# A decode step of a hybrid layer on one core: low products moved to the end of each unit, one head's convolution moved to VectorE

## The chip, the core and the metric

The kernel runs on one core of a Trainium2 chip, in one launch. Its time is the device time of an execution in microseconds (us). TensorE is called PE here, VectorE DVE, ScalarE ACT, GpSimd POOL and SyncE SP, as in the profile. Every engine works off its own list of instructions in order; a wait for another engine or for a DMA stops that list.

## The reference

One layer of a decoder trunk for 256 prompt and 64 sample tokens (8 sequences of 8), 320 columns in all, with a model width of 2048, in fp32:

```
h = rmsnorm(x)
proj = h @ w_in                       # 2048 x 3072: a_val, a_gate, b_u, b_v, c_u
z = a_val * sigmoid(a_gate)           # A: 4 heads of 128 channels
out_a = silu(layernorm_heads(depthwise_conv31(concat[state, z]) + conv_b))
out_b = b_u * (tril(w_s) @ layernorm(b_v) + b_s)          # B: 4 heads of 128
out_c = s5(c_u)                       # C: 64 groups of 16 channels, a complex diagonal SSM, then a GLU
x = x + concat[out_a, out_b, out_c] @ w_out
g, u = split(rmsnorm(x) @ w_gu)       # 2048 x 11264
x = x + (silu(g) * u) @ w_down        # 5632 x 2048
y = rmsnorm(x)
```

Returned are y, the convolution's last 30 positions, the SSM's last states and the layer-normed b_v rows of the samples. The depthwise convolution has 31 taps per channel: each output position is the sum of 31 shifted copies of the row, each with its channel's weight.

## The kernel before

**Products.** Activations lie with channels on partitions and the 320 tokens along the row. Every weight matrix comes from memory as tiles of 128x1024 fp32 (a *unit*: eight 128x128 blocks, `j` = 0 to 7). To keep fp32 accuracy a product is made of three passes: ACT rounds the weights to `hi` (line 208), DVE makes the remainder `lo` = raw - hi (line 217, recorded as L52, the line of the helper through which all DVE work goes), and the activation rows are kept as a high and a low part as well. For block `j` PE does `hi` x high row (L237), `hi` x low row (L238) and `lo` x high row (L240), all into one PSUM tile `acc`. In `mm` (line 232) a unit is done in four quarters of two blocks: four matmuls with `hi`, then two with `lo`.

**Order.** Loads, splits and products of unit u+3, u+2, u+1 and u are issued side by side from one loop over the units. `ORDER` (line 26) lists the units of the mixers after the first eight: C0 to C7 are the SSM's inputs, A2 and A3 the convolution heads 2 and 3 (heads 0 and 1 come first), K0 to K3 the convolutions of the four heads, U0 to U3 and V the two halves of B. After them come 16 output tiles for the C channels (`post_oc`), 16 for A and B, the gate/up tiles and the down tiles.

**Work beside the products.** The mixers' own work is written as generators (`Task`). `Side.run` is called after each quarter of a unit. Tasks of priority below 1 are stepped whenever they are due; `Wait(n)` makes a task due n quarters later. Tasks of priority 1 and up (the SSM's recurrence, layer norms, B's gating) are stepped while the estimated time of the DVE work issued so far (`vec.t`) is not above that of the PE work (`pe`, line 131). `side.until(cond)` steps every task that is due, without that limit, until the condition holds. All of this happens while the program is built: it fixes the order of each engine's list, and not a time.

**Convolution.** `conv_in` (line 544) writes a head's row to DRAM and reads it back four times, shifted, into `z4` (32 channels x 4 shifts on 128 partitions, issued from POOL). `k_mm` (line 565) then does the 31 taps as eight groups of four on PE with 32x32 diagonal weights `cwd`; `k_post` adds the bias.

**The C chain.** `c_out` (three PE products per group) gives `z`, ACT applies gelu, `z_layout` (line 927) turns it through DRAM (`dz`, then four reads into `zc`, all issued from SP), `c_glu` (line 937) does two PE products, ACT the tanh, DVE the product `oc`, ACT its high part `oh` and DVE its low part `ol`. The first C output tile needs all eight such pairs of rows (`crows`).

**End.** After the last product the final norm's factor multiplies 16 rows of `xa`: rows 12 to 15 on POOL (two operations), the others on DVE, with seven stores (line 1366).

## Time and profile before

| what | us |
|---|---|
| median of 3 runs | 1352.18 (1348.64, 1352.18, 1353.87) |
| the profiled execution | 1352.68 |
| its span, first to last instruction | 1351.0 |
| PE busy in the span | 1318.4 |
| DVE busy | 721.8 |
| ACT busy | 565.8 |
| PE idle in the first 296 us, all of it | 18.3 |
| PE idle between 296 us and the last down product | 0.0 |

The profile is of one execution. Its time stands against the span: 1.7 us lie outside. The idle time of PE was read off the timeline row by row (waits of 0.3 us and more; the last of them before the final norm ends at 295.15 us). A busy PE is not always a PE at full speed: the granted clock is 1.00 in nearly every stretch, and lower in a few of the first 225 us.

### The profile page before, as it was taken

To read this page: it belongs to the slowest core of one execution; us is meant where nothing else is said; L and a number is where in the kernel's file an instruction comes from. 1 tells how busy PE (TensorE), PEld (TensorE's weight loads), DVE (VectorE), ACT (ScalarE), POOL (GpSimd) and SP (SyncE) were. 2 spreads that over 40 slices of the span, in tenths; PEclk is the share of its full clock that TensorE was granted. 3 is DMA by queue.
4 is the path that set the end of the run, shared out by engine and by line. 5 is a ranking of instruction groups with operands and counts; after the bars stand their busy time and mean duration, and the time that the engine had idled before them with its cause. 6 is when DMAs were issued, how large, how long until landed. Compare 5 with 4: busy or idle time off the path is not lost.

```text
span 1351.0 us, 22667 instructions
## 1 busy us (share of the span) xinstructions
PE 1318.4 (98%) x9324; PEld 1290.4 (96%) x9324; DVE 721.8 (53%) x1195; ACT 565.8 (42%) x824; POOL 71.9 (5%) x101
## 2 busy tenths in 40 slices
PE   8999999999999999999999999999999999999995
PEld 8888987899999999999999999999999999999995
DVE  8867986685555444444444444444444444434444
ACT  7378535474454333333333333333233333322452
POOL 1110101010130000000000000000000000000112
PEclk9999998999999999999999999999999999999998
DMA  7784576564444554444444444555444445554453
GB/s 261 194 204 133 142 187 161 168 210 141 149 147 142 175 173 148 148 141 157 155 146 151 141 157 155 147 150 152 146 156 145 152 141 158 155 148 141 142 152 121
DMA packets 78584, 212.49 MB, mean 157 GB/s; under 512 B 20640, under 2 KB 28064, under 8 KB 78416
## 3 DMA queue, kind: packets, MB, share of 16 engines
q1 hardware_dynamic: 71440, 198.34, 46.6%
q0 software_dynamic: 6176, 10.94, 3.2%
q8 instruction: 73, 1.20, 0.4%
q10 hardware_dynamic: 864, 1.76, 0.3%
q14 instruction: 31, 0.25, 0.1%
HBM read 203.47 MB, written 8.73 MB: 157 GB/s over the span
## 4 chain that ended last, share of the span: by engine, by line
PE 90%; DVE 4%; DMA 3%; ACT 2%; issue 1%; SPq 0%; DVEq 0%; ACTq 0%
PE acc L240 28%; PE acc L237 28%; PE acc L238 28%; DMA raw<-in_win 2%; DVE lo L52 1%; PE acc L577 1%; PE sc L758 1%; PE sc L914 1%; PE acc L1018 1%; PE sc L915 1%; PE sc L916 1%; PE acc L1020 1%; PE acc L1019 1%; PE sc L770 0%; ACT hi L208 0%
## 5 line engine op out<-in xcount | busy, mean ns | idle before, releaser
L52 DVE TENSOR_TENSOR lo<-raw,hi 128x1024 fp32r<-128x1024 f32 (+1 forms) x357 | 421.3, 1181 | 213.5 <-issue 164.0
L208 ACT ACTIVATE hi<-raw 128x1024 fp32r<-128x1024 f32 (+2 forms) x361 | 369.3, 1024 | 340.1 <-PE acc L238 246.5
L237 PE MATMUL acc<-hh,hi 128*128 128x320 f32 x1408 | 424.4, 309 | 0.0
L238 PE MATMUL acc<-hl,hi 128*128 128x320 f32 x1408 | 422.8, 308 | 0.0
L240 PE MATMUL acc<-hh,lo 128*128 128x320 f32 x1408 | 321.0, 308 | 0.0
L237 PEld LDWEIGHTS acc<-hh,hi 128*128 128x128 f32 x1408 | 264.4, 188 | 0.1
L238 PEld LDWEIGHTS acc<-hl,hi 128*128 128x128 f32 x1408 | 264.4, 188 | 0.1
L240 PEld LDWEIGHTS acc<-hh,lo 128*128 128x128 f32 x1408 | 234.7, 188 | 0.0
L237 PE MATMUL acc<-fh,hi 128*128 128x320 f32 x704 | 212.0, 309 | 0.0
L238 PE MATMUL acc<-fl,hi 128*128 128x320 f32 x704 | 211.8, 308 | 0.0
L240 PE MATMUL acc<-fh,lo 128*128 128x320 f32 x704 | 165.5, 308 | 0.0
L237 PEld LDWEIGHTS acc<-fh,hi 128*128 128x128 f32 x704 | 132.2, 188 | 0.0
L238 PEld LDWEIGHTS acc<-fl,hi 128*128 128x128 f32 x704 | 132.1, 188 | 0.0
L240 PEld LDWEIGHTS acc<-fh,lo 128*128 128x128 f32 x704 | 118.9, 188 | 0.0
L52 DVE TENSOR_TENSOR xa<-acc,xa 128x320 f32<-128x320 f32 x80 | 39.3, 491 | 127.8 <-PE acc L240 127.8
L237 PE MATMUL acc<-xh,hi 128*128 128x320 f32 x288 | 91.2, 324 | 2.0 <-ACT hi L208 2.0
L1210 ACT ACTIVATE fh<-fu 128x320 fp32r<-128x320 f32 x44 | 20.8, 472 | 163.0 <-DVE fu L52 163.0
L238 PE MATMUL acc<-xl,hi 128*128 128x320 f32 x288 | 87.8, 312 | 0.0
L1188 ACT ACTIVATE fg<-fg 128x320 f32<-128x320 f32 x44 | 20.8, 472 | 138.9 <-DVE fg L52 138.9
L52 DVE TENSOR_TENSOR fu<-acc,rs 128x320 f32<-128x320 f32 x44 | 21.6, 492 | 98.0 <-PE acc L240 98.0
L52 DVE TENSOR_TENSOR fg<-acc,rs 128x320 f32<-128x320 f32 x44 | 21.6, 492 | 95.9 <-PE acc L240 95.9
L240 PE MATMUL acc<-xh,lo 128*128 128x320 f32 x288 | 66.9, 314 | 4.4 <-DVE lo L52 4.4
(255 smaller groups left out, 1353.5 us busy)
## 6 DMA issues: line engine op xcount, KB each, us to landing
raw<-in_wgu SPq DMA_DIRECT2D x176, 512.0 KB, 3.5
raw<-in_wdn SPq DMA_DIRECT2D x80, 512.0 KB, 3.6
raw<-in_win SPq DMA_DIRECT2D x37, 512.0 KB, 4.5
raw<-in_wout SPq DMA_DIRECT2D x32, 512.0 KB, 3.5
z<-zr POOLq DMA_DIRECT2D x16, 296.0 KB, 12.6
raw<-in_wv SPq DMA_DIRECT2D x8, 512.0 KB, 4.2
raw<-in_wdn SPq DMA_DIRECT2D x16, 256.0 KB, 2.6
xa<-in_xT SPq DMA_DIRECT2D x4, 640.0 KB, 7.5
```

Source lines behind the costliest of these rows:

```text
L52: return self.v.tensor_tensor(out, a, b, op=op)
L208: A.activation(d["hi"][:, o], d["raw"][:, o], AF.Copy)
L237: T.matmul(ps, hi[:, c], r[u + j][0], start=u + j == 0, stop=False)
L238: T.matmul(ps, hi[:, c], r[u + j][1], start=False, stop=False)
L240: T.matmul(ps, lo[:, j * 128:j * 128 + 128], r[u + j][0], start=False, stop=u + j == n - 1)
L577: T.matmul(ps[c, o:o + n], w[:, 32 * (8 * g + j):32 * (8 * g + j) + 32], x, start=j == 0, stop=j == 7, tile_position=(0, 32 * g))
L758: T.matmul(pe[:, 80 * p:80 * p + 80], ps[ri][:, p, :], U[:, ct, p, :], start=True, stop=True)
L914: T.matmul(o, cat(bd[:, 0, p, 1:5]), H[:, 0, 4 * i + p, 0:80], start=True, stop=False)
L915: T.matmul(o, cat(bd[:, 1, p, 1:5]), H[:, 1, 4 * i + p, 0:80], start=False, stop=False)
L916: T.matmul(o, Tt[:, p, :], U[:, i, p, :], start=False, stop=True)
L1188: A.activation(gs, gs, AF.Silu)
L1210: A.activation(h, ub, AF.Copy)
```

## The change

Seven edits. Where a block of eight had been worked off in four quarters of `hi, hi, hi, hi, lo, lo`, the unit's 16 products with `hi` now come first and its eight with `lo` last. K3 is gone from `ORDER`: the fourth head is convolved in `conv_v` on DVE, 31 taps of one operation on 256 and one on 64 columns, as a task of priority 3.5; its weights are a small table `cw`, and its row goes to the output straight from SBUF. `conv_in` waits two quarters before each of its four shifted reads. `Side.run` lets DVE's estimate run 2.0 us ahead of PE's. `dz` is written from ACT's queue at once; the reads back come five quarters later instead of four, and are due after four instead of three. `b_load` comes after head 2's convolution. The last 16 rows are all multiplied on DVE, in six operations, with six stores.

```diff
-ORDER = "C0 C1 C2 C3 K0 C4 C5 C6 C7 K1 A2 U0 A3 U1 K2 V K3 U2 U3".split()
+ORDER = "C0 C1 C2 C3 K0 C4 C5 C6 C7 K1 A2 U0 A3 U1 K2 V U2 U3".split()
...
-        while self.vec.t <= self.pe:
+        while self.vec.t <= self.pe + 2.0:
...
-                for j in range(a, b):
-                    c = slice(j * 128, j * 128 + 128)
-                    T.matmul(ps, hi[:, c], r[u + j][0], start=u + j == 0, stop=False)
-                    T.matmul(ps, hi[:, c], r[u + j][1], start=False, stop=False)
-                for j in range(a, b):
-                    T.matmul(ps, lo[:, j * 128:j * 128 + 128], r[u + j][0], start=False, stop=u + j == n - 1)
+                todo = [(hi, j, i) for j in range(m) for i in range(2)] + [(lo, j, 0) for j in range(m)]
+                for w, j, i in todo[3 * a:3 * b]:
+                    T.matmul(ps, w[:, j * 128:j * 128 + 128], r[u + j][i], start=w is hi and u + j + i == 0,
+                             stop=w is lo and u + j == n - 1)
...
-            side.add(0.3, conv_in(h))
+            if h < 3:
+                side.add(0.3, conv_in(h))
+            else:
+                side.add(3.2 + 0.1 * h, conv_v(h))
...
         for g in range(4):
+            yield Wait(2)
             G.dma_start(z4[:, g], bass.AP(tensor=base.tensor, offset=base.offset + 32 * g * ZW,
                                            ap=[[1, 4], [ZW, 32], [1, Z4]]))
+
+    def conv_v(h):
+
+        row, cw = S["row", h], S["cw"]
+        G.dma_start(O["rows"][h], row)
+        while "cw" not in S or S["of"] >= 7:
+            yield Wait(1)
+        S["of"] += 1
+        f = tmp("of", bufs=7)
+        fs = f[:, NP:].rearrange("p (s t) -> p s t", s=8)
+        for k in range(31):
+            w = cw[:, k:k + 1]
+            for o, x in ((f[:, 0:NP], row[:, k:k + NP]), (fs, samples(row)[:, :, k:k + 8])):
+                if k == 0:
+                    V.tensor_scalar(o, x, w, cv[:, h, 0:1], op0=MULT, op1=ADD)
+                else:
+                    V.scalar_tensor_tensor(o, x, w, o, op0=MULT, op1=ADD)
+            yield None
+        S["k", h] = True
+        side.add(0.9, mix_a(h, f))
...
-            if h == 3:
+            if h == 1:
+                side.until(lambda: "src" in S)
+                cw = S["cw"] = tmp("kk", (128, 64))
+                G.dma_start(cw[:, 0:32], I["cw"])
+            if h == 2:
                 b_load()
...
-        yield Wait(2)
-        nc.sync.dma_start(dz, z)
-        yield Wait(4)
+        nc.scalar.dma_start(dz, z)
+        yield Wait(5)
         for p in range(4):
             nc.sync.dma_start(zc[32 * p:32 * p + 32], dz[:, p, :].rearrange("(j g) q -> g j q", j=4))
-        S["z due", i] = side.now + 3
+        S["z due", i] = side.now + 4
...
-        if u in (100, 102, 104, 106):
+        if u in (100, 102, 104):
...
-    for E, q, a, b in ((G, 3, 0, 2), (G, 3, 2, 4), (V, 0, 0, 1), (V, 0, 1, 4), (V, 1, 0, 4), (V, 2, 0, 3), (V, 2, 3, 4)):
-        E.tensor_tensor(rows(q, a, b), rows(q, a, b), r[:, None, :].to_broadcast([128, b - a, NT]), op=MULT)
-    for E, q, a, b in ((nc.sync, 0, 0, 1), (nc.scalar, 0, 1, 4), (nc.sync, 3, 0, 2), (nc.scalar, 1, 0, 4),
-                       (nc.sync, 3, 2, 4), (nc.scalar, 2, 0, 3), (nc.sync, 2, 3, 4)):
-        E.dma_start(O["yT"][:, 4 * q + a:4 * q + b, :], rows(q, a, b))
+    for n, (q, a, b) in enumerate(((0, 0, 1), (0, 1, 4), (1, 0, 4), (2, 0, 4), (3, 0, 3), (3, 3, 4))):
+        V.tensor_tensor(rows(q, a, b), rows(q, a, b), r[:, None, :].to_broadcast([128, b - a, NT]), op=MULT)
+        (nc.scalar if n % 2 else nc.sync).dma_start(O["yT"][:, 4 * q + a:4 * q + b, :], rows(q, a, b))
```

What this does to the engines' lists, at the three places that the next sections speak of.

**PE, from the last quarters of U3 to the first C output tile.** Before, `sc<-zc,wg` (the two GLU products of a group) and `sc<-z,wv` (B's mixing product of a head) have parts of U3 (`acc<-xh,hi` and so on) between them; `sm<-of` is a sum for the layer norm of a convolution head:

```order
L606 MATMUL sm<-of,ones_113 128x320
L237 MATMUL acc<-xh,hi 128x320
L238 MATMUL acc<-xl,hi 128x320
L237 MATMUL acc<-xh,hi 128x320
L238 MATMUL acc<-xl,hi 128x320
L240 MATMUL acc<-xh,lo 128x320 x2
L1064 MATMUL sc<-z_3185,wv 128x128
L1065 MATMUL sc<-z_3185,wv 128x128
L1066 MATMUL sc<-z_3185,wv 128x64
L949 MATMUL sc<-zc,wg 128x320
L950 MATMUL sc<-zc,wg 128x320
L1064 MATMUL sc<-z_3185,wv 128x128
```

Now the same place reads:

```order
L237 MATMUL acc<-xh,lo 128x320 x6
L974 MATMUL sc<-zc,wg 128x320
L975 MATMUL sc<-zc,wg 128x320
L1089 MATMUL sc<-z_2586,wv 128x128
L1090 MATMUL sc<-z_2586,wv 128x128
L1091 MATMUL sc<-z_2586,wv 128x64
L624 MATMUL sm<-of,cent 128x320
L974 MATMUL sc<-zc,wg 128x320
L975 MATMUL sc<-zc,wg 128x320
L1089 MATMUL sc<-z_2586,wv 128x128
L1090 MATMUL sc<-z_2586,wv 128x128
L1091 MATMUL sc<-z_2586,wv 128x64
```

With K3 gone the units end sooner in the list: the last two GLU products and the last two mixing products stand behind the whole of U3, with no unit's products between them, and the first C output tile follows at once.

**DVE, at the end of V.** Before, the recurrence's last addition (`H<-lnv`) is followed by the reads of V's sums (`wv<-acc`):

```order
L52 TENSOR_TENSOR lnv<-lnv,H 128x256
L52 TENSOR_TENSOR H<-lnv 128x2x16x8
L61 TENSOR_SCALAR wv<-acc,rc 128x512
L52 TENSOR_TENSOR wv<-acc,wv 64x512
L52 TENSOR_TENSOR lo<-raw,hi 128x1024
```

Now six taps (`of<-row,kk`, a 256 and a 64 each) stand between them; here the last two of them:

```order
L56 SCALAR_TENSOR_TENSOR of<-row,kk,of 128x256
L56 SCALAR_TENSOR_TENSOR of<-row,kk,of 128x64
L56 SCALAR_TENSOR_TENSOR of<-row,kk,of 128x256
L56 SCALAR_TENSOR_TENSOR of<-row,kk,of 128x64
L61 TENSOR_SCALAR wv<-acc,rc 128x512
L52 TENSOR_TENSOR wv<-acc,wv 64x512
L52 TENSOR_TENSOR lo<-raw,hi 128x1024
```

**DVE, before the last low C row.** Now, from the product `oc` of group 7 to its low row `ol<-oc,oh`:

```order
L56 SCALAR_TENSOR_TENSOR oc<-g_3440,g_3439 128x4x80
L56 SCALAR_TENSOR_TENSOR of<-row,kk,of 128x256
L56 SCALAR_TENSOR_TENSOR of<-row,kk,of 128x64
L52 TENSOR_TENSOR gs<-sc,z_2586 128x256
L52 TENSOR_TENSOR gs<-sc,z_2586 128x64
L56 SCALAR_TENSOR_TENSOR of<-row,kk,of 128x256
L56 SCALAR_TENSOR_TENSOR of<-row,kk,of 128x64
L52 TENSOR_TENSOR ol<-of,oh 128x320
L52 TENSOR_TENSOR ol<-oc,oh 128x320
```

Before, the same two had an inverse square root's two operations between them:

```order
L56 SCALAR_TENSOR_TENSOR oc<-g_3468,g_3467 128x4x80
L56 SCALAR_TENSOR_TENSOR is_3454<-is_3456,is_3454 128x320
L52 TENSOR_TENSOR is_3454<-sm,is_3454 128x320
L52 TENSOR_TENSOR ol<-oc,oh 128x320
L52 TENSOR_TENSOR gs<-sc,z_3185 128x256
```

Of the 31 taps, 6 stand before V's sums are read, 5 between that and the layer norm of V (`ic<-mv,ic`), 13 between there and the last low C row, and 7 after it.

POOL's list: the four shifted reads of heads 0 and 1 (`z<-zr`) still follow each other directly in it, one small load stands before the fourth read of head 2, the four reads of head 3 are gone, and B's tables with the first of their masks (affine selects, L991 before) have come forward to the place behind head 2's reads, which is in V's stretch.

## Rows read from the trace of the kernel before

**Rows 1.** The page: busy time of the engines, and the chain's shares.
```profile
PE 1318.4 (98%) x9324; PEld 1290.4 (96%) x9324; DVE 721.8 (53%) x1195; ACT 565.8 (42%) x824; POOL 71.9 (5%) x101
...
PE 90%; DVE 4%; DMA 3%; ACT 2%; issue 1%; SPq 0%; DVEq 0%; ACTq 0%
```

Windows have these columns: from and to, length, then the busy time of PE, PEld, DVE, ACT and POOL with their instructions, the clock granted to PE, the busy share of the DMA engines, and GB/s.

**Rows 2.** Windows: a stretch of the gate/up tiles.
```profile
1000.00:1200.00 200.00, 200.00 (x1367) 200.00 (x1366) 91.77 (x106) 67.99 (x78) 0.00 (x0) 1.00 0.48 151
```

**Rows 3.** PE's waits: what waited for what; us, times, longest.
```profile
PE acc L240 <- DVE lo L52: 4.4, 5, 1.6
...
PE acc L237 <- ACT hi L208: 2.0, 2, 1.2
PE sc L949 <- issue: 1.9, 1, 1.9
...
PE sc L240 <- DVE lo L52: 0.6, 2, 0.4
```

**Rows 4.** PE's timeline: start, us; in brackets the wait ahead and its releaser.
```profile
34.52 0.56 PE L240 MATMUL acc<-xh,lo 128*128 128x320 f32 x2 [1.56 <-DVE lo L52]
...
213.44 0.78 PE L949 MATMUL sc<-zc,wg 128*128 128x320 f32 x2 [1.88 <-issue]
```

**Rows 5.** Windows: five us behind the first wait, ten behind the second.
```profile
35.00:40.00 5.00, 5.00 (x36) 5.00 (x35) 4.86 (x11) 2.18 (x2) 0.00 (x0) 1.00 0.66 209
215.00:220.00 5.00, 5.00 (x28) 4.86 (x31) 0.00 (x0) 0.46 (x1) 0.59 (x1) 0.50 0.80 201
220.00:225.00 5.00, 5.00 (x26) 3.81 (x26) 2.10 (x8) 3.33 (x11) 0.00 (x0) 0.53 0.26 89
```

**Rows 6.** POOL's timeline: the four shifted reads of head 3.
```profile
202.57 2.75 POOL L556 DMA_DIRECT2D z<-zr  x4 [14.19 <-PE acc L577]
```

**Rows 7.** The page, DMA issues: KB each, us from issue to landing.
```profile
z<-zr POOLq DMA_DIRECT2D x16, 296.0 KB, 12.6
```

**Rows 8.** Windows: end of V to the last low C row; its second part.
```profile
251.56:295.10 43.54, 42.00 (x388) 37.61 (x387) 28.00 (x53) 28.63 (x49) 6.38 (x15) 1.00 0.66 212
268.75:295.10 26.35, 25.50 (x167) 23.41 (x166) 22.20 (x43) 21.38 (x35) 4.76 (x12) 1.00 0.71 235
```

**Rows 9.** PE's timeline: the products of K3.
```profile
255.11 2.80 PE L577 MATMUL acc<-z,hi 128*32 128x256 f32 x48 [0.69 <-DVE wv L61]
...
261.25 1.96 PE L577 MATMUL acc<-z,hi 128*32 128x256 f32 x80
```

**Rows 10.** DVE's timeline, from head 3's row to the last low C row.
```profile
186.93 0.56 DVE L56 SCALAR_TENSOR_TENSOR row<-gs,rs 128x256 f32<-128x256 f32 x2
187.40 1.22 DVE L52 TENSOR_TENSOR lo<-raw,hi 128x1024 fp32r<-128x1024 f32 x1
...
268.75 0.16 DVE L56 SCALAR_TENSOR_TENSOR ic<-mv,ic 128x3 f32<-128x3 f32 x1 [6.92 <-ACT ic L311]
...
294.62 0.48 DVE L52 TENSOR_TENSOR ol<-oc,oh 128x320 fp32r<-128x320 f32 x1
```

**Rows 11.** DVE's operations by form: us in total, mean ns; idle before.
```profile
L56 DVE SCALAR_TENSOR_TENSOR row<-gs,rs 128x256 f32<-128x256 f32 x4 | 1.7, 425 | 0.1
...
L56 DVE SCALAR_TENSOR_TENSOR row<-gs,rs 128x64 f32<-128x64 f32 x4 | 0.9, 218 | 0.0
```

**Rows 12.** Timeline of DVE and POOL: affine selects and products on 512 columns.
```profile
268.98 1.62 POOL L991 TENSOR_SCALAR_AFFINE_SELECT z<-z 128x128 f32<-128x128 f32 x5 [4.34 <-DMA z<-in_wst]
...
270.82 1.36 DVE L52 TENSOR_TENSOR wv<-wv,lnv 128x512 f32<-128x512 f32 x2
...
273.24 2.48 DVE L52 TENSOR_TENSOR wv<-wv,lnv 128x512 f32<-128x512 f32 x4
```

**Rows 13.** DVE's and POOL's timeline: the last products.
```profile
1339.40 7.10 DVE L52 TENSOR_TENSOR xa<-xa,rs 128x320 f32<-128x320 f32 x5
...
1339.44 4.24 POOL L1367 TENSOR_TENSOR xa<-xa,rs 128x640 f32<-128x640 f32 x2 [7.29 <-DVE rs L56]
```

**Rows 14.** DVE's operations by form: one product on 1280 columns.
```profile
L52 DVE TENSOR_TENSOR H<-H,U 128x1280 f32<-128x1280 f32 x1 | 1.5, 1486 | 0.0
```

More of the change, by code (lines that the diff above doesn't have):

```diff
@@ L561, in f @@
             side.until(lambda: ("z4", h) in S)
-            S["kps", h] = acc()
+            S["kps", h] = sc() if h == 3 else acc()
         return f
@@ L1399, in layout @@
     cw[:31] = f["conv_w"][0]
+    a["cw"] = np.zeros((128, 32), np.float32)
+    a["cw"][:, :31] = f["conv_w"][0][:, 384:].T
     cwd = np.zeros((4, 4, 32, 4, 8, 32), np.float32)
```

2 lines of the change are left out of this document (1 added, 1 removed).

## The prediction

> **What bounds the kernel now.** I read the page's first and fourth part first. PE is busy for 1318.4 of 1351.0 us and holds 90% of the chain that ended last; DVE is at half [rows 1]. So an engine other than PE matters only where PE waits for it. The windows come next: in the gate/up stretch PE is busy for 200.00 us of 200.00 and starts 1367 matmuls, 146.3 ns each, at clock 1.00 [rows 2], with VectorE (DVE) busy for 91.77. From 296 us to the last product PE has no wait. The order of passes inside a unit cannot make that part quicker: a unit has 24 matmuls before and after, each as long. Three places are left in which the time can change: the waits before the end of V, the stretch from V's end to the first C output tile, and the last 12 us after the products. The reader is to look there in PE's waits and its timeline, and in windows for what each engine has to do in the stretch.
>
> **A. Before V's end.** The low passes. PE waits 4.4 and 0.6 us in seven waits for DVE's remainder `lo`, the longest 1.6 [rows 3]. A unit's first `lo` product comes after 16 matmuls where it came after 4: 12 x 0.146 = 1.76 us later, longer than the longest wait. Were `lo` made at the same time as before, all 5.0 would go. But DVE's estimate may now run 2.0 us ahead, so tasks of priority 1 and up may stand before a `lo` where they stood behind it, above all from 130 us on. With the waits as they are, between the two, nearer the full sum: -3.5, bounds -1.8 (one unit's worth of delay) and -5.0.
>
> The spaced reads. `hi` is late twice, 2.0 us in all [rows 3], and I put that down to raw weights that land late beside a head's four shifted reads (no row shows it). `Wait(2)` spaces reads in program order, but nothing of PE's pace holds POOL: its list for heads 0 and 1 is still four reads in a row, and four issue in 2.75 us [rows 6]. So the burst stays: -0.5, bounds 0 and -2.0.
>
> The fourth head's reads. At 213.44 PE waits 1.88 us for `zc`, its releaser given as issue, since a DMA is what is late [rows 4]. Head 3's reads were issued at 202.57 and took 12.6 us to land in the median [rows 6, 7], so they were under way just then. In ten us behind this wait the clock granted is 0.50 and 0.53 [rows 5], the level of 1.2 GHz instead of 2.4. At half clock a stretch does half its work: 5.00 x 0.50 + 5.00 x 0.47 = 4.85 us lost. Wait and clock together are 6.7. The head's row now stays in SBUF, these four reads do not exist, `dz` is issued by ACT without its two-quarter wait, and `zc` is due one quarter later. I take -6.0, bounds 0 (the wait is B's tables' or the `dz` trip's own) and -6.7.
>
> What the new order adds: the variance product of a head stands six matmuls earlier, 6 x 0.146 = 0.9, if the operation it waits for does not come sooner as well; and B's tables with their masks now fall into V's stretch, 0 to 1. Taken together +1.0, bounds 0 and +1.9. ACT's queue gets the `dz` store: behind it stand the `hi` roundings, and the store waits for the gelu, which is ACT's own and is done by then; so nothing. Sum of A: -3.5 - 0.5 - 6.0 + 1.0 = -9.0.
>
> A rule that speaks against A is in the Trainium skill, page "SBUF — State Buffer", section "Who interferes with whom": a DVE operation with two SBUF inputs and a GpSimd operation exclude each other on a shared port. Eight masks in V's stretch, beside the recurrence, would by it cost up to their own length, 8 x 0.32 = 2.6 (five take 1.62 [rows 12]). The trace shows less: two products on 512 columns beginning while the masks ran took 1.36 together, 0.68 each, and four of them soon after 2.48, 0.62 each [rows 12]; 0.06 for each product is within my +1.0.
>
> **B. From V's end to the first C tile.** V's last product ends at 251.56, the low row that the C tile needs at 295.10: 43.5 us. PE is busy for 42.00 of them [rows 8]. K3's 128 matmuls, 2.80 and 1.96 long [rows 9], less the overlap of their ends, are 4.7, and they go. PE's own work is then 42.00 - 4.7 = 37.3. If PE alone set the end, this stretch would give back over 4 us.
>
> But DVE takes K3's place. A tap is one operation on 256 and one on 64 columns of the same kind as head 3's `row`: their own durations are 425 + 218 = 643 ns [rows 11], and from the start of such a pair to the next instruction 187.40 - 186.93 = 0.47 [rows 10]. I take 0.52, bounds 0.47 and 0.64. All 31 are 16.1 us. Six stand before the sums of V are read, and five before V's layer norm, where DVE waits 6.92 us for ACT anyway [rows 10]; these eleven (5.7) are hidden but for the wait of U2's first products on those sums, which is off the chain that I follow. 13 stand between the layer norm and the last low row, 7 behind it. The layer norm's point `ic` was at 268.75, 17.2 us after V's end; U2's products in K3's place put it about 1 us earlier, 16.2. From there DVE had 26.35 us, 22.20 of them busy [rows 8]. Out of its list before the last low row go one `lo` (1.22) and three operations of 0.49 on 320 columns (about the 0.48 of the low row), in come a pair `gs` (of the shape of the pair that takes 0.56)  and two low rows of 0.48 [rows 10]: 22.20 - 2.69 + 1.52 = 21.0. The 13 taps make it 21.0 + 13 x 0.52 = 27.8. With no idle time the last low row is ready 16.2 + 27.8 = 44.0 us after V's end, with all of the former idle time (26.35 - 22.20 = 4.15) at 48.2. DVE is the tighter engine now and has more to choose from, so I take 1.0 of idle: 45.0, which is +1.5 against 43.5. What is late next is thus DVE, 7 us behind PE's own work.
>
> Two more terms. After the last low row PE formerly had two `lo` products left of that unit; now all eight stand behind it: 6 x 0.146 = +0.9. And since the last units end before the GLU products of the list's end, PE's spare time of 45.0 - 37.3 = 7.7 us lies in one or two waits instead of being spread. After the wait of 1.88 the clock fell for ten us [rows 4, 5]; behind one of 1.56, the longest `lo` wait of all, it stayed at 1.00 [rows 3 to 5]. I take +1.5, bounds 0 and 4.85, since some of what runs slow there lies under DVE's time. Sum of B: 1.5 + 0.9 + 1.5 = +3.9.
>
> The Trainium skill, page "TensorE: Matmul & The Clock Gate", section "Why this matters for your kernels", warns of idle gaps between bursts of products, which send the clock to its lower level. The fall behind 213.44 agrees, the wait at 34.52 shows a gap without one. By that rule the full 4.85 would be due and the sum would be 3.4 higher.
>
> **The tail.** DVE's five operations on 12 of the 16 rows fill 7.10 us from 1339.40, with POOL beside it for 4.24 [rows 13]. Now DVE has all 16: two rows alone at 0.48 to 0.49 and 14 in operations priced by the one on 1280 columns, 1.486 or 0.37 a row [rows 14]: 0.98 + 5.20 = 6.2. So -0.9, bounds 0 (the stores wait for the memory and not for DVE) and -1.25.
>
> **Sum.** -9.0 + 3.9 - 0.9 = -6.0 against the profiled execution's 1352.68: 1346.7. It ran 0.5 above the median of the three, so as a run 1346.
>
> **Rivals.**
> 1. The taps are hidden. DVE takes its taps in the idle time it has, 4.15 in that stretch and 6.92 ahead of it, and PE's own 37.3 us plus a short wait decides. The stretch shrinks by 3.4 instead of growing by 3.9: about 1340 (1336 to 1342). For it: DVE is at 53% overall. Against it: from 268.75 on it is busy for 22.20 of 26.35 already.
> 2. The removed wait comes back. Without head 3's reads, `zc` is still late at 213 (its trip through memory is its own, or the loads of B take the queues), and the half clock with it: -6.0 does not happen, 1352.5. For it: the releaser is "issue", and no row names the reads as the cause. Against it: the other groups' `zc` did not make PE wait 1.88, and head 3's was the only burst under way there.
> 3. Slower: DVE's chain from V's layer norm is so late that it outweighs A. Its place is the wait of PE for the last low C row. Prices: taps at 0.64 (+1.6), all of the former idle kept (+3.1), PE falling to the lower clock in the wait for it (+3.4), and `lo` late behind DVE's tasks (+1.7): 1346.5 + 9.8 = 1356; with the reads' gain halved as well 1359, and with all of it gone 1362. It decides from the point where the last low row is more than 9 us later than the 43.5 of before. For it: DVE's list there has no slack but the idle time. Against it: it needs several ends of the bounds on one chain.
>
> **How the numbers follow.** Forecast 43%, own range 1341 to 1350; rival 1 25%; rival 2 19%; rival 3 13%. The range 1336 to 1358 reaches from rival 1 to the near edge of rival 3. About 0.5%, or 6.8 us, is what a measurement of this kernel can tell from no change: faster means below 1345.4, slower above 1358.9. Faster: rival 1 whole (0.25) and not quite half of the forecast (0.19), 0.44. Slower: rival 3, 0.13. The same: the rest, 0.43.
>
> **What the profile after would show.** A right: PE's waits for `lo` fall below 2 us in all, those for `hi` stay near 2; no wait near 213 us, and windows behind it at 1.00. B right: `ic` about 16 us after V's end, the last low row about 45, DVE busy for almost all of the time between, taps 0.47 to 0.64 apart, and PE waiting some 7 us in a few waits for DVE. The tail right: 6.2 us from the first to the last product of the final norm. I am wrong in the mechanism if PE's idle time in the stretch after V is below 3 us (rival 1), if a wait for `zc` with a low clock behind it is still there (rival 2), or if a new wait that stands nowhere above costs more than 3 us.

## The result, and the profile after

The changed kernel is slower: 1361.28 us in the median of its first four runs (1355.36 to 1361.93) against 1350.75 in four of the kernel before, a ratio of 1.0073 (95% interval 1.0044 to 1.0102). The forecast was 1346 and the range 1336 to 1358. Its profiled execution took 1355.36 us, 2.7 more than that of before; its timed ones lie near 1361. That difference is taken up below, since it turned out to be the main thing.

The first two rows of the page of the changed kernel that answer to [rows 1]:

```profile
PE 1315.8 (97%) x9196; PEld 1290.9 (95%) x9196; DVE 738.3 (55%) x1258; ACT 561.3 (41%) x824; POOL 65.5 (5%) x96
...
PE 87%; DVE 7%; DMA 3%; ACT 2%; issue 1%; SPq 0%; DVEq 0%; ACTq 0%; POOLq 0%
```

PE has 128 matmuls fewer and is busy for 2.6 us less, and the span is 2.7 us longer: it stands idle for 5.3 us more. PE's waits after, which answer to [rows 3] (us in total, times, longest):

```profile
PE acc L237 <- ACT hi L208: 3.1, 1, 3.1
PE sc L940 <- DVE H L52: 2.7, 1, 2.7
...
PE sc L900 <- ACT m L722: 2.2, 1, 2.2
PE sc L1089 <- DVE gs L52: 2.1, 1, 2.1
PE sm L632 <- ACT of L629: 2.0, 1, 2.0
PE sm L624 <- ACT of L608: 2.0, 1, 2.0
PE sc L974 <- issue: 1.8, 1, 1.8
...
PE acc L237 <- DVE lo L52: 1.1, 1, 1.1
```

The reader is to look at the last column. Before, one wait of the list was 1.8 us or longer (1.88), and the waits for `lo` were seven. Now `lo` costs one wait, and eight waits are 1.8 to 3.1 us long (the seven long rows here and one of 1.9 for ACT's `H`). The idle time was not taken away; it grew, and it stands in longer pieces.

What stands behind the long pieces is in the windows of the changed kernel (columns as ahead of [rows 2]; the third number from the right is the clock):

```profile
60.00:80.00 20.00, 16.90 (x200) 14.72 (x199) 12.38 (x38) 4.23 (x4) 0.26 (x1) 0.91 0.85 198
80.00:95.00 15.00, 10.93 (x61) 10.08 (x61) 9.25 (x22) 13.10 (x25) 2.69 (x4) 0.89 1.05 218
...
185.00:205.00 20.00, 16.19 (x117) 14.90 (x119) 16.68 (x43) 8.31 (x15) 0.00 (x0) 0.91 0.50 143
215.00:220.00 5.00, 5.00 (x47) 4.37 (x47) 4.49 (x20) 1.84 (x7) 2.25 (x6) 1.00 0.68 238
220.00:225.00 5.00, 5.00 (x23) 3.95 (x22) 3.89 (x10) 3.73 (x10) 2.59 (x6) 1.00 0.65 186
250.00:270.00 20.00, 18.72 (x125) 17.83 (x124) 14.18 (x35) 7.07 (x14) 1.62 (x3) 0.91 0.49 156
280.00:295.00 15.00, 10.92 (x57) 8.69 (x56) 14.79 (x40) 10.58 (x20) 0.54 (x1) 0.89 0.81 281
295.00:310.00 15.00, 15.00 (x92) 14.77 (x91) 9.79 (x21) 6.18 (x9) 0.00 (x0) 0.88 0.22 72
```

The low clock at 215 to 225 us [rows 5] is gone, as forecast. In its place the clock is 0.88 to 0.91 in the six other windows, each with a wait of 1.3 to 3.1 us in it or just ahead of it. A window of 20 us at 0.91 has lost 20 x 0.09 = 1.8 us, one of 15 us at 0.89 1.65: the losses come in pieces of about this size, or of twice that.

The length of a wait is no safe sign of what follows it. The kernel before has such a piece behind a wait of 1.16 us too:

```profile
65.85 0.41 PE L237 MATMUL acc<-xh,hi 128*128 128x320 f32 x1 [1.16 <-ACT hi L208]
```

```profile
65.00:70.00 5.00, 3.74 (x17) 3.48 (x18) 3.51 (x10) 1.85 (x2) 0.00 (x0) 0.77 0.78 241
70.00:75.00 5.00, 5.00 (x32) 5.00 (x32) 4.62 (x21) 1.06 (x1) 0.00 (x0) 0.89 0.71 173
```

That is 5 x 0.23 + 5 x 0.11 = 1.7 us lost, and behind a wait of 1.40 us at 98.17 it is as much (0.84 and 0.82 in the windows from 95 to 105 us), whereas behind the wait of 1.56 us [rows 4, 5] there was nothing. In the changed kernel the wait of 2.04 us at 84.70 and the one of 2.20 at 241.39 have full clock behind them. Over two profiles of the kernel before and five of the changed one, from 20 us on, the clock falls in or within 2.6 us behind 27 of the 36 waits of 1.8 us or more, and 4 of the 25 waits of 1.1 to 1.8 us. Behind a long wait a fall is much likelier, but neither certain nor confined to it.

**Clock lost.** Every run has its span and its mean granted clock, so the same sum can be made for runs without a profile: span x (1 - clock). The clock is given to three digits, so one run is known to 0.7 us and a median moves in steps of 0.7 to 1.35. For 10 runs of the changed kernel its median is 22.4 us, for 33 of the kernel before on the same chip 10.8. What is left of the span is 1336.7 and 1338.0. By this sum the whole difference is clock lost. It is a sum and not yet a cause, since a low clock costs nothing where PE waits for another engine anyway. (By the windows of the last 15 us some 5 us of the loss lie behind the last product in either profile, where no product is slowed.) The profiled executions show less of it than the timed ones: five profiles of the changed kernel are at 1354.96 to 1355.93 with 16 to 20 us lost, nine timed runs at 1357.5 to 1366.3 with 23.1 in the median. Which waits cost the timed runs the further 5 us is in no trace of this kernel. A profile of the nearest other one, without the spacing of the reads, took 1358.69 us with 24 lost: its low stretches lie at the same places, but at 66 us (there 70) and at 196 us 3.4 us are lost in place of 1.7.

**Where the profile's 2.7 us arise.** The start of the same product in both, in us:

| product | before | after | difference |
|---|---|---|---|
| second unit of `w_in` | 13.99 | 15.18 | +1.2 |
| 15th unit | 65.85 | 63.31 | -2.5 |
| 19th unit | 89.87 | 94.91 | +5.0 |
| 26th unit | 143.88 | 147.81 | +3.9 |
| first `c_out` product behind V | 251.56 | 253.14 | +1.6 |
| end of the last low C row | 295.10 | 298.92 | +3.8 |
| first product of the final norm | 1335.14 | 1339.27 | +4.1 |
| last instruction | 1351.0 | 1353.7 | +2.7 |

Up to the 15th unit the low passes give what was forecast: 3.7 us between the second unit and this one. From there to the 19th unit 7.6 us are lost. The tail gives 1.4 us. The stretch behind V costs 2.2 us up to the last low row.

DVE's timeline of the changed kernel behind V answers to [rows 10]:

```profile
271.06 0.16 DVE L56 SCALAR_TENSOR_TENSOR ic<-mv,ic 128x3 f32<-128x3 f32 x1 [3.96 <-ACT ic L309]
...
295.24 0.68 DVE L56 SCALAR_TENSOR_TENSOR of<-row,kk,of 128x256 f32<-128x256 f32 x2
295.83 0.74 DVE L56 SCALAR_TENSOR_TENSOR oc<-g,g 128x320 f32<-128x320 f32 x1
...
298.43 0.49 DVE L52 TENSOR_TENSOR ol<-oc,oh 128x320 fp32r<-128x320 f32 x1
```

A tap takes 295.83 - 295.24 = 0.59 us (0.52 was taken); `ic` comes 17.9 us after V's end and not 16.2; the last low row 45.8 after it (45.0 was forecast). DVE is the chain there, as the forecast had it. The window of the stretch answers to [rows 8], and the tail's row to [rows 13]:

```profile
253.14:299.20 46.06, 40.70 (x255) 37.61 (x254) 38.83 (x97) 28.09 (x48) 2.29 (x5) 0.89 0.54 177
```

```profile
1343.53 5.83 DVE L52 TENSOR_TENSOR xa<-xa,rs 128x320 f32<-128x320 f32 x6
```

PE is busy for 40.70 us there, not 37.3: part of it ran at the lower clock (0.89 of 46 us is 5 us lost). From `ic` to the last low row DVE is busy for 27.5 of 27.9 us, so what PE loses there lies under DVE's time. The 16 rows take DVE alone 5.83 us, where DVE and POOL together needed 7.10; the 0.9 forecast was 1.3.

### The profile page after: what moved, and what is told of

Read it like the earlier page. It is cut to its first block, busy times and chain, and to the rows that moved or that the text cites. A ratio compares the mean times of both kernels' runs of the same rounds, so it can differ in the third digit from the quotient of the medians.

```text
span 1353.7 us, 22453 instructions
## 1 busy us (share of the span) xinstructions
PE 1315.8 (97%) x9196; PEld 1290.9 (95%) x9196; DVE 738.3 (55%) x1258; ACT 561.3 (41%) x824; POOL 65.5 (5%) x96
## 4 chain that ended last, share of the span: by engine, by line
PE 87%; DVE 7%; DMA 3%; ACT 2%; issue 1%; SPq 0%; DVEq 0%; ACTq 0%; POOLq 0%
PE acc L237 82%; DMA raw<-in_win 2%; DVE lo L52 2%; DVE lnv L52 1%; PE sc L237 1%; PE sc L784 1%; DVE H L52 1%; PE sc L940 0%; PE sc L942 0%; PE sc L941 0%; ACT hi L208 0%; DVE xa L52 0%; DVE wv L52 0%; DVE of L56 0%; PE acc L599 0%
## 5 line engine op out<-in xcount | busy, mean ns | idle before, releaser
L208 ACT ACTIVATE hi<-raw 128x1024 fp32r<-128x1024 f32 (+2 forms) x360 | 363.4, 1023 | 266.3 <-PE acc L237 186.4
L237 PE MATMUL acc<-hh,hi 128*128 128x320 f32 x1408 | 416.0, 309 | 0.0
L237 PE MATMUL acc<-hl,hi 128*128 128x320 f32 x1408 | 415.6, 308 | 0.0
L237 PEld LDWEIGHTS acc<-hl,hi 128*128 128x128 f32 x1408 | 264.4, 188 | 0.1
L237 PEld LDWEIGHTS acc<-hh,hi 128*128 128x128 f32 x1408 | 264.4, 188 | 0.1
L237 PE MATMUL acc<-hh,lo 128*128 128x320 f32 x1408 | 235.2, 308 | 0.0
L237 PEld LDWEIGHTS acc<-hh,lo 128*128 128x128 f32 x1408 | 213.6, 188 | 0.0
L237 PE MATMUL acc<-fh,hi 128*128 128x320 f32 x704 | 207.4, 309 | 0.0
L237 PE MATMUL acc<-fl,hi 128*128 128x320 f32 x704 | 207.2, 308 | 0.0
L237 PEld LDWEIGHTS acc<-fl,hi 128*128 128x128 f32 x704 | 132.2, 188 | 0.0
L237 PEld LDWEIGHTS acc<-fh,hi 128*128 128x128 f32 x704 | 132.2, 188 | 0.0
L237 PE MATMUL acc<-fh,lo 128*128 128x320 f32 x704 | 118.3, 308 | 0.0
L237 PEld LDWEIGHTS acc<-fh,lo 128*128 128x128 f32 x704 | 106.7, 188 | 0.0
L237 PE MATMUL acc<-xh,hi 128*128 128x320 f32 x288 | 92.3, 333 | 4.4 <-ACT hi L208 3.1
L237 PE MATMUL acc<-xl,hi 128*128 128x320 f32 x288 | 89.1, 322 | 0.0
L237 PEld LDWEIGHTS acc<-xh,hi 128*128 128x128 f32 x288 | 57.4, 199 | 6.8 <-ACT hi L208 3.9
```

The lines of the kernel that those rows point to most:

```text
L208: A.activation(d["hi"][:, o], d["raw"][:, o], AF.Copy)
L237: T.matmul(ps, w[:, j * 128:j * 128 + 128], r[u + j][i], start=w is hi and u + j + i == 0, stop=w is lo and u + j == n - 1)
```

## The experiments

Each kernel was timed in turns with the kernel before on one chip; four more runs are single profiled executions. The table has the medians, the ratio to the kernel before with its interval, the clock lost, and the rest of the span (medians each, so they need not add up). The changed kernel was timed beside the next three of the table; the other differences to it go across chips, on which the kernel before stands at 1351.0 to 1351.4. The mean of a row has a standard error of 0.4 to 1.7 us, so most differences of under 2 us are not told from noise.

| kernel | us | ratio (95%) | lost | rest |
|---|---|---|---|---|
| before (27 to 33 runs a chip) | 1351.0 to 1351.4 | | 10.8 | 1338 |
| changed, again | 1361.1 | 1.0069 (1.0048, 1.0091) | 22.4 | 1336.7 |
| changed, no spacing | 1358.6 | 1.0038 (1.0017, 1.0059) | 22.4 | 1334.3 |
| changed, K3 on PE | 1360.3 | 1.0061 (1.0042, 1.0080) | 17.6 | 1340.9 |
| changed, 0 ahead | 1354.2 | 1.0016 (0.9999, 1.0033) | 16.2 | 1336.1 |
| changed, no low-last | 1355.0 | 1.0026 (1.0011, 1.0042) | 16.2 | 1337.0 |
| changed, old dz | 1364.2 | 1.0084 (1.0055, 1.0113) | 22.5 | 1340.2 |
| changed, no spacing, 0 ahead | 1352.1 | 1.0001 (0.9986, 1.0016) | 16.2 | 1333.9 |
| changed, waits filled | 1357.6 | 1.0042 (1.0027, 1.0057) | 12.9 | 1342.5 |
| before + low-last | 1352.1 | 1.0020 (0.9996, 1.0044) | 16.9 | 1336.9 |
| before + 2.0 ahead | 1353.1 | 1.0013 (0.9998, 1.0027) | 12.8 | 1338.4 |
| before + taps, dz, tail | 1349.3 | 0.9988 (0.9976, 1.0001) | 13.5 | 1334.1 |
| the same + spacing | 1352.1 | 1.0007 (0.9989, 1.0025) | 13.5 | 1337.0 |
| the same three, one wait filled | 1350.3 | 0.9994 (0.9978, 1.0010) | 10.8 | 1337.6 |
| before + dz, tail | 1349.8 | 0.9988 (0.9974, 1.0002) | 9.4 | 1337.8 |

The theories that the expectations name: 1, the spaced reads cost it; 2, the taps on DVE; 3, the 2.0 us that DVE's estimate may run ahead; 4, formed on the first four runs, the low clock behind longer waits.

**The changed kernel again.** No edit.

> The changed kernel once more, beside the next three on one chip. Its first four times were 1355.36 (the profiled one) and three near 1361.5. All theories: median 1355 to 1362. If this profile falls near 1361, the 6 us that the first profile does not show must stand in it as one more wait or a stretch at the lower clock; the place decides which edit made it. If all runs are near 1355, the three near 1361 were the other chip or moment.

Measured: 1361.1 in the median of 10 runs, the profiled one 1354.96. Not the chip nor the moment; the profiled execution again shows less than the timed ones.

**No spacing.**

```diff
         for g in range(4):
-            yield Wait(2)
             G.dma_start(z4[:, g], ...
```

> The changed kernel without the two-quarter wait ahead of each shifted read. Theory 1 (the spacing put head 0's burst behind a row load on POOL that waits 2.1 us, and split head 2's): head 0's four reads go out near 51.4 us instead of 54.4, the wait of 3.10 us for hi at 70 us falls to about 1, PE reaches the units of 80 to 95 us some 2.7 us sooner, head 2's fourth read goes out with the third, the wait of 2.71 us at 194 and the low clock behind it go: 5 us faster than the changed kernel (3 to 8). Theory 2 (the taps on DVE cost it): within 2 us of the changed kernel. Theory 3 (the 2.0 us that DVE's estimate may run ahead): within 2 us, with the wait at 194 us still there.

Measured: 2.6 us faster than the changed kernel. The burst went out earlier, as expected. POOL's timeline, the changed kernel first, then without spacing:

```profile
53.89 0.54 POOL L542 DMA_DIRECT2D row<-in_rows  x1 [2.11 <-DMA zr<-row]
54.42 2.75 POOL L558 DMA_DIRECT2D z<-zr  x4
```

```profile
52.29 2.75 POOL L557 DMA_DIRECT2D z<-zr  x4
55.03 0.59 POOL L542 DMA_DIRECT2D row<-in_rows  x1
```

With `Wait(2)` a row load that waits 2.11 us for a store to land stands ahead of all four reads: nothing was spaced, the burst only came later. But the wait for `hi` at 70 us did not go, it stood ahead of the unit before and was longer:

```profile
67.50 0.63 PE L237 MATMUL acc<-xh,hi 128*128 128x320 f32 x1 [3.64 <-ACT hi L208]
```

So theory 1 fails as the main cause; the 2.71 at 194 us stayed as well. In three pairs of the table the spacing costs 2.6, 2.1 and 2.8 us, each pair's intervals overlapping; where, is open.

**K3 back on PE.**

```diff
-ORDER = "... K1 A2 U0 A3 U1 K2 V U2 U3".split()
+ORDER = "... K1 A2 U0 A3 U1 K2 V K3 U2 U3".split()
...
-            if h < 3:
-                side.add(0.3, conv_in(h))
-            else:
-                side.add(3.2 + 0.1 * h, conv_v(h))
+            side.add(0.3, conv_in(h))
```

> The changed kernel with the fourth head's convolution back on PE (K3 in the order, its shifted reads, B's tables after K3). Theory 1: the loss up to 95 us stays (the wait for hi at 70 us near 3, PE 5 us behind the kernel before at 95 us); after V it gains 3.1 us on DVE and gives back nothing on PE, but the wait near 213 us with the low clock behind it comes back: within 3 us of the changed kernel. Theory 2: the taps are the cost, so 5 us or more faster, no slower than the kernel before. Theory 3: within 2 us.

What goes with K3 goes back too: head 3's reads, and B's tables behind K3.

Measured: 0.9 us faster than the changed kernel. Theory 2 falls. The wait near 213 us, which theory 1 expected back with the reads, is not there (the two products stand at 213.90 with nothing ahead). The two columns say why the taps neither gain nor lose: the rest grows by 4.2 us, which is K3's time on PE (4.7 by [rows 9]), and the clock lost shrinks by 4.8.

**0 ahead.**

```diff
-        while self.vec.t <= self.pe + 2.0:
+        while self.vec.t <= self.pe:
```

> The changed kernel with DVE's estimate held to PE's, as before (0 instead of 2.0 us ahead). Theory 3: ACT's kpad stands ahead of the late hi again, DVE's idle time of 5.6 us at 180 to 186 us and PE's wait of 2.71 at 194 go: 4 us faster. Theory 1: the waits at 70, 85 and 89 us stay, since no task of priority 1 stands there; within 2 us. Theory 2: within 2 us.

Measured: 6.9 us faster than the changed kernel, almost all of it clock lost (22.4 to 16.2). Theory 3 names an edit that costs. At the place it spoke of, ACT's `kpad` stands directly behind a `hi` that comes 5 us late; the changed kernel first, then with 0 ahead:

```profile
184.52 1.06 ACT L208 ACTIVATE hi<-raw 128x1024 fp32r<-128x1024 f32 x1 [5.03 <-PE acc L237]
185.49 0.23 ACT L911 ACTIVATE kpad<-sc 128x96 f32<-128x96 f32 x1
```

```profile
179.77 1.06 ACT L208 ACTIVATE hi<-raw 128x1024 fp32r<-128x1024 f32 x1 [5.18 <-DMA raw<-in_win]
180.74 0.23 ACT L911 ACTIVATE kpad<-sc 128x96 f32<-128x96 f32 x1
```

With 2.0 ahead `kpad` stands behind the 42nd `hi` of ACT's list, with 0 ahead behind the 41st. DVE's next operation needs it and waits 5.63 us (3.80 with 0 ahead), the recurrence behind that comes late, and PE waits 2.71 us for its `H` at 194 us with the clock at 0.91 behind it (the window from 185 us above). With 0 ahead the wait for `H` is still there, 1.80 us at 197.15, but the window of the same time is at full clock:

```profile
185.00:205.00 20.00, 16.03 (x146) 13.92 (x144) 18.23 (x46) 7.59 (x10) 0.00 (x0) 1.00 0.54 176
```

It is not the idle time alone that differs: PE is idle for 4.0 us there, as against 3.8, but in shorter pieces, the longest 2.10. So `kpad` alone does not explain the gain: that product even begins 2.8 us later with 0 ahead. From it to the first `c_out` product behind V the changed kernel then takes 3.7 us more; it has 1.7 us of low clock there and a wait of 2.20 us for ACT's `m` at 241 (0.57 here), and the rest is not traced.

**No low-last.** L237 to L240 as in the kernel before.

```diff
-                todo = [(hi, j, i) for j in range(m) for i in range(2)] + [(lo, j, 0) for j in range(m)]
...
+                for j in range(a, b):
+                    T.matmul(ps, lo[:, j * 128:j * 128 + 128], r[u + j][0], start=False, stop=u + j == n - 1)
```

> The changed kernel with each quarter's lo products back behind its own hi products. Theory 4, formed on the first runs (at full clock the changed kernel would be no slower; the time goes in stretches at the lower clock behind PE's waits of about 2 us, which are more now): the waits for lo come back as several of under 1.6 us, PE reaches the stretch limited by transfers at 63 to 95 us later and waits less there; the clock lost (span times one less the granted clock) falls from 22 to about 17 us, and the time by some 4 us to 1357. Theory 3 (only the 2.0 us ahead costs): clock lost stays near 22, and the time is 1360 to 1363.

Measured: 6.2 us faster than the changed kernel, the whole of it clock lost (22.4 to 16.2), as theory 4 had it (it expected 4). But not where it had it: from the 15th to the 19th unit (64.4 to 95.5 us) this kernel takes as long as the changed one, 31.1 us against 30.8 to 32.0.

**Old dz.** `dz` from SP behind `Wait(2)`, the reads after `Wait(4)`.

> The changed kernel with dz written from SP two quarters later and read back as before. All theories: within 2 us of the changed kernel (1359 to 1363); if dz on ACT's queue or the later reads cost something, a gain of over 3 us and a smaller wait for zc at 290 us would show it.

Measured: 3.1 us slower than the changed kernel (6 runs), in the rest and not in the clock; the two intervals overlap, so it is not clear of noise. In its profile PE waits 7.28 us for `zc` at 301 us, where the longest such wait in the first profile of the changed kernel is 1.82. The new way of `dz` seems to pay, which no theory had said; which of its three parts does is open.

**Before with low-last alone.** The reverse of the edit of no low-last.

> The kernel before with the low products at the end of each unit and nothing else. My prediction's term: 3.5 us faster than before (1348). Theory 4: the waits for lo go (PE 3 us ahead at 63 us) and come back as longer waits behind the transfers at 63 to 95 us, with 2 to 4 us more clock lost than the 10.8 of before: 1350 to 1354, no gain.

Measured: 1.1 us slower than before in the median and not 3.5 faster, with an interval that reaches from level to 0.4% slower. Its runs scatter from 1348.8 to 1365.4, and the medians of the parts (rest -1.1, clock lost +6.1) do not add up to that of the whole; by the means it is 2.9 +- 1.5 slower, 3.8 +- 1.1 more clock lost and 0.9 +- 1.1 less rest. Its profile shows the start as one of the places (the first row), where the products of the second unit came 1.1 us later than before, and 185 us as another:

```profile
10.00:20.00 10.00, 10.00 (x53) 10.00 (x54) 9.35 (x35) 6.00 (x14) 0.00 (x0) 0.76 1.03 383
...
185.00:205.00 20.00, 17.30 (x164) 14.44 (x166) 19.52 (x50) 6.30 (x11) 0.59 (x1) 0.91 0.52 169
```

In the kernel before the same windows are at 0.85 and 1.00.

**No spacing and 0 ahead.** Both edits above.

> The changed kernel without the two-quarter waits and without the 2.0 us ahead. If the two add up (2.6 and 7.0 us by the medians): 1351.5, level with the kernel before. If they act on the same waits: 1354, as without the 2.0 us alone. Theory 4: whatever the time, span less lost clock stays at 1334 to 1337 and the time follows the clock lost, here 14 to 18 us.

Measured: 1352.1, so the two add up (9.1 against 2.6 + 6.9), and the kernel is level with the one before. Low-last is still in it, and 16.2 us are lost.

**Waits filled.** Nothing is removed; 40 idle products go into PE's list ahead of five of the long waits.

```diff
+    def fill(ps, n):
+        for _ in range(n):
+            T.matmul(ps, cent, cent, start=True, stop=True)
...
         yc = sm()
+        if h == 0:
+            fill(yc[:, 0:128], 8)
         T.matmul(yc[:, :NT], cent, f, start=True, stop=True)
```

> The changed kernel with 40 idle products (128 columns of a constant, into PSUM columns that the next product overwrites) in PE's list at five places where it waited about 2 us in both profiles: 8 and 5 ahead of head 0's two layer-norm sums, 11 ahead of the first c_out, 9 inside the last product of masks, 7 ahead of the last GLU. At 0.22 us each they fill most of each wait and take no wait away. Theory 4 (the time goes at the lower clock behind those waits): the clock lost falls from 22 to about 14 to 16 us, the time by 5 to 8 to about 1354. Rival (the waits themselves cost, the clock is by the way): no faster than 1361, and up to 2 slower where a filled wait would have been shorter.

Measured: 3.5 us faster than the changed kernel, although it does some 10 us more of work on PE (the five rows of idle products take 1.61 + 1.27 + 2.62 + 3.13 + 1.72): the clock lost falls by 9.5 (22.4 to 12.9), the rest rises by 5.8. By the means it is 4.0 +- 1.2 us faster. That is the clearest of the runs: no engine gets its data sooner, and still the time falls. Its windows:

```profile
80.00:95.00 15.00, 11.42 (x81) 10.49 (x79) 7.47 (x19) 12.13 (x23) 0.00 (x0) 1.00 1.06 222
95.00:120.00 25.00, 22.14 (x170) 20.80 (x169) 16.68 (x41) 22.37 (x50) 2.04 (x3) 0.86 0.43 120
185.00:205.00 20.00, 19.33 (x161) 17.93 (x159) 17.32 (x43) 9.34 (x15) 0.00 (x0) 1.00 0.52 159
...
280.00:295.00 15.00, 12.40 (x77) 10.46 (x76) 14.79 (x40) 11.08 (x20) 1.69 (x3) 1.00 0.84 287
295.00:310.00 15.00, 13.03 (x76) 12.39 (x75) 9.68 (x24) 6.53 (x11) 0.00 (x0) 0.89 0.19 66
```

At four of the five places (in the windows from 80, 185 and 280 us) the clock stays at 1.00, where it was 0.89 to 0.91; at 95 to 120 and behind 295 us, whose waits were not filled, it still falls. The fifth place missed: the idle products among the masks came behind the wait for `m` and not ahead of it, the wait stayed, and behind it the clock fell:

```profile
PE sc L910 <- ACT m L730: 2.3, 1, 2.3
```

```profile
235.00:256.00 21.00, 18.74 (x95) 14.83 (x94) 16.34 (x37) 8.41 (x19) 0.35 (x1) 0.92 0.44 132
```

PE's timeline shows one filled wait (at 194 us, 2.71 before; the 22 records are 11 idle products, two each) and one that was left:

```profile
192.50 2.62 PE L621 MATMUL sc<-cent 128*128 128x128 f32 x22
195.29 0.45 PE L952 MATMUL sc<-H,m 128*128 128x80 f32 x2 [0.17 <-DVE H L52]
```

```profile
294.60 0.46 PE L1103 MATMUL sc<-z,wv 128*128 128x128 f32 x2 [2.00 <-DVE gs L52]
```

The gain was forecast at 5 to 8: one place of five missed, and the idle products cost more than the waits that they filled.

**Before with three edits: taps, dz, tail.**

> The kernel before with three of the edits alone: the fourth head's convolution on DVE, dz from ACT, the tail. No low-last, no spacing, no 2.0 us ahead. If the parts add up as their removals did (low-last 6.2, ahead 7.0, spacing 2.6 of 1361.1): 1346, some 5 faster than before. Theory 4: clock lost back at about 11, the rest 1334 to 1336: 1346 to 1348. If low-last and ahead act on the same waits: 1351 to 1352, no gain over before.

B's tables stay ahead of time here, with the taps that made room for them.

Measured: 1349.3, 11.8 us faster than the changed kernel and 1.7 faster than before, which its interval does not quite bear out. It has 13.5 us lost and the lowest rest but one. The removals do not add up: by their sum it would have been 1346.

**Before with 2.0 ahead alone.** The reverse of the edit of 0 ahead.

> The kernel before with DVE's estimate allowed 2.0 us ahead and nothing else. Theory 3 (this edit costs by itself, through longer waits for ACT and DVE with the low clock behind them): clock lost 15 to 18 instead of 10.8, the time 1355 to 1358. Rival (it costs only together with the taps or low-last): within 2 us of before.

Measured: 2.1 us slower, 2.0 of it clock lost, with an interval that just reaches level: between theory and rival. Alone it costs 2, beside the other edits 6.9.

**The kernel before, a second profile.**

> The kernel before, for a second profile of it: the waits below 1.6 us behind which the clock stayed, and the one of 1.88 behind which it fell, are expected at the same places, with some 8 to 13 us of clock lost in all.

Measured: 1357.39 us. Two waits were far longer than in the first profile:

```profile
PE sc L770 <- issue: 4.5, 1, 4.5
PE sc L949 <- issue: 2.7, 1, 2.7
```

The loss of 12 us is as expected, the places are not: at 66 us the wait is 1.08 and nothing is lost behind it, where the first profile lost 1.7. So single profiles of one kernel differ by 5 us, through waits for transfers, and a difference of 2.7 between two of them says little.

**Three more profiles of the changed kernel.**

> The changed kernel, for its profile. Theory 4: 14 to 24 us of clock lost, each piece of 1.6 to 3.5 us behind a wait of PE of about 2 us: at 70, 85 to 95, 103, 194, 241, 257, 290 to 293 us. A place that loses clock in this look and not in the first two had its wait in those too. Rival: a place without any wait ahead of it loses clock.

> The changed kernel, for one more profile. Theory 4: the same places lose clock as in the profiles before it, some more and some less, and what differs in the time is the number of places. Rival: a place without any wait ahead of it.

> The changed kernel, for the last profile. Theory 4: the same places, each behind a wait of about 2 us; over five profiles the places behind V lose more than before did. Rival: the loss stands in one stretch alone, at 60 to 120 us.

Measured: 1355.93, 1355.40, 1355.18. Three places lose clock in all five profiles: the start, 60 to 120 and 289 to 300 us. From 185 to 200 us four of them do, at 241 or 257 four. Each piece has a wait of 1.2 us or more ahead of it; 12 to 15 us are lost in all up to 340 us. No stretch alone has it. But a wait does not bring the loss each time. The one of 2.71 us for `H` is in the second profile as in the first, and there the clock stays:

```profile
195.23 0.42 PE L940 MATMUL sc<-H,m 128*128 128x80 f32 x2 [2.71 <-DVE H L52]
```

```profile
180.00:200.00 20.00, 16.94 (x127) 16.25 (x119) 14.43 (x36) 8.02 (x13) 0.00 (x0) 1.00 0.75 194
```

The gate/up tiles begin 4.3 to 5.2 us later than in the first profile of before in all five. None fell near 1361, so what the timed runs lose further stays open.

**Before with dz and tail.**

> The kernel before with dz from ACT and the tail alone, K3 on PE. Theory 4: K3's 4.7 us on PE come back as time at full clock (rest 1337 to 1338 instead of 1334.1) and the waits that the taps leave go, so less clock is lost than the 13.5 of the three edits: 9 to 11. Time 1347 to 1350, within 2 us of the three edits. Rival (the taps pay): 1352 or more.

Measured: 1349.8, level with the three edits: the taps give 3.7 us in the rest and take 4.1 in the clock. In its profile PE has no wait at 213 us at all, although K3 and head 3's four reads (at 204.84) are in it. Nor has it one in the profile of before with low-last alone, which has the reads (at 206.28) and the old `dz`: the two products stand at 215.10 with nothing ahead.

**The three edits with the spacing.**

> The three edits (taps on DVE, dz from ACT, tail: 1349.3) with the spaced reads. If spacing costs by itself (2.6 and 2.1 us were seen by taking it away): 1351 to 1352, with head 0's burst starting at 54 us instead of 51. Rival (it cost only beside low-last or the 2.0 us ahead): within 1 us of 1349.3.

Measured: 1352.1, 2.8 slower, all in the rest. The burst starts at 55.45 us in place of 52.70.

**The three edits with one wait filled.** Ten idle products ahead of the last GLU.

> The three edits with ten idle products (2.2 us in all) ahead of the last GLU, where PE waited 2.53 us with 1.6 us of clock lost behind it. Theory 4: clock lost 11.5 to 12.5 instead of 13.5 and the rest up by less than 1: 1347.5 to 1349. Rival (the clock there costs nothing since DVE sets the end): 1349 to 1350.5.

Measured: 1350.3. The clock lost falls by 2.7, the rest rises by 3.5: no gain, as the rival had it. In the profile of the three edits that wait is 2.53 us:

```profile
286.55 1.09 PE L975 MATMUL sc<-zc,wg 128*128 128x320 f32 x2 [2.53 <-issue]
```

Where this single wait is filled the idle products cost what the clock gives.

**What the runs add up to.** In a row they lead from one kernel to the other: before with dz and tail 1349.8, with the taps 1349.3, with the spacing 1352.1, with the 2.0 us ahead 1355.0 (the table's "no low-last"), with low-last 1361.1. The last two steps can be taken the other way round, by "0 ahead" at 1354.2. So, from 1352.1, the 2.0 us ahead cost 2.9 alone, low-last 2.1 alone, and both 9.0, of which 8.9 is clock lost (13.5 to 22.4). By the means 4.3 +- 1.5 us belong to the pair and to neither alone; the removals of 6.9 and 6.2 each hold them. Where the two meet no profile shows.

## Why the prediction was wrong

**The step that failed is the sum of A, -9.0.** It counted the waits that the edits take away, put what the same edits make of the waits that stay at +1.0, and put the clock behind those at nothing. Between the profiles of the two kernels A came out at +1.6 to +3.7 against the first one of before (and at -3.1 to -1.0 against the second, which is 4.7 us later there). In the timed runs low-last and the 2.0 us ahead, priced together at -3.5, cost 9.0 us, 8.9 of it clock lost.

*The low passes (-3.5).* Up to 63 us the term was right: 3.7. Where low-last stands without the spacing and without the 2.0 us, it held still further: the 20th unit begins 82.7 and 83.6 us after the second in those two profiles, 86.1 in before and 87.6 in the three edits. In the changed kernel it is 88.8 to 90.5, of which 30.8 to 32.0 are from the 15th to the 19th unit (24.0 before). That is not low-last alone: with it alone these four units take 25.0, and the changed kernel without it takes 31.1. The profiles with the spaced reads take 26.8 to 32.0 there, those without 23.7 to 27.4; what makes it is open. In the timed runs low-last gains nothing all the same: in three pairs without the 2.0 us, by the means, the rest moves by -0.9, +0.4 and -1.2 us, none of it clear of noise, and 1.8 to 3.8 us more are lost in the clock.

*The clock.* The prediction priced it at two places, as 4.85 given back at 213 us and 1.5 paid behind V: -3.4 in all. Measured: +11.6 (10.8 to 22.4). It held the waits of 1.56 us to be harmless and the one of 1.88 to be not [rows 4, 5], but the same trace has 1.7 us lost behind waits of 1.16 and 1.40 us, and it did not ask what the edits would make of the others. With low-last the short waits for `lo` go and PE meets a late `hi` in one long wait instead (3.10 us, or 2.35 with low-last alone, where before had 1.16); with 2.0 us ahead background work of ACT and DVE stands differently to what PE needs (`kpad`, `m`). Such a piece of about 2 us with 1.7 us of clock behind it costs nearly double. The wait of 2.71 us for `H` with 1.7 of clock is a new wait of over 3 us, which the prediction had named as a sign of a wrong mechanism. The Trainium skill's warning of idle gaps (page "TensorE: Matmul & The Clock Gate", section "Why this matters for your kernels") was weighed at the one wait in B; by the windows above it bore on most of the long waits that A made. The clock also fell behind waits of 1.2 to 2.7 us, which are shorter than the gaps that the page warns of.

*The 2.0 us ahead* was given no term of its own but only a shade on the low passes. It is the edit that, taken out, gives back most: 6.9.

*Head 3's reads (-6.0).* The wait at 213 us and the low clock behind it did go. But the reason given does not hold: three kernels with the four reads in place have no such wait either, one of them with the old `dz`. Rival 2's doubt, that no row names the reads as the cause, was right; what made `zc` late there is open, and the time came back in other waits (2.71 at 194, 2.20 at 241 us).

*What the new order adds (+1.0)* was too small. The two layer-norm sums of head 0 wait for ACT for 2.04 + 2.04 us and waited 0.72 before: +3.4 by themselves, above the bound of 1.9. The prediction's reading of [rows 12] on the shared port is also too strong: the five masks end at 268.98 + 1.62 = 270.60, ahead of the two products at 270.82, so only a sixth mask (0.54 us from 271.10) ran beside these.

*The spaced reads (-0.5).* That POOL isn't held to PE's pace was right; that the order stays was read off for heads 0 and 1 and held to be harmless, though a row load had come ahead of the burst. It costs 2 to 3 us.

**B (+3.9) held in sign and engine, and in its number in part by luck.** From V's end to the gate/up tiles the first profile of the changed kernel loses 4.67 - 1.58 = 3.1 us, the four others 1.5 to 1.9. DVE's chain decides (27.5 us of work from `ic`, 27.8 forecast), and the taps eat what K3 gave. The single terms were off in both directions (`ic` 1.7 later, taps 0.07 dearer each, less idle time).

**The tail (-0.9) held:** 1.4 from the last sum to the end.

The slower rival had the right place for part of it, but its mechanism (one late low row) is not what decided: with dz and tail alone the taps leave the kernel level (1349.3 against 1349.8).

## What to carry to other kernels

On an engine that is busy for 98% of the time, ask of every edit not only how much waiting it removes but how long the pieces are that remain: here a wait of about 2 us had mostly, and a shorter one seldom, 1.7 us or more of low clock behind it, and then cost about double. Look for such losses behind all waits of the trace that one has, the short ones too. A low clock is seen in runs without a profile, as span times what is missing from the mean granted clock, and that sum told where to look: the changed kernel's span less its clock lost was no longer than before. Removing edits one by one counted 4 us twice here; two kernels with one of the two edits each and one with neither showed it.

## What the runs showed of the hardware

Filling a wait with idle products kept the clock at 1.00 at four places of five; 40 products took 9.5 us from the clock lost, and the rest grew by 5.8 us. The same wait of 2.71 us had 1.7 us of low clock behind it in one execution of a kernel and none in another. Profiled executions of the changed kernel lose 16 to 20 us of clock and the timed ones 23; no trace of it shows where. DVE alone multiplies the 16 last rows in 5.83 us; with POOL beside it on four of them (4.24 us), DVE took 7.10 for the other 12: POOL's help cost more than it gave.
